# A linear attention kernel on one core: the first four pairs' output stored by eight software DMAs of 1 MB instead of four of 2 MB

## The chip, the core and the metric

The kernel runs on one core of a Trainium2 chip. The metric is the device time of one execution in microseconds (us), the median of three runs. Besides these there is one execution that was taken by the hardware profiler; everything that is said of single instructions and DMAs comes from that one.

## The reference, cut to what matters

Q, K and V are float32 arrays of 8 x 12 heads x 512 rows x 64 columns, 12.58 MB each; the output has the same shape. The computation is attention without a softmax:

```python
Q_feat = np.maximum(0, Q) + 1
K_feat = np.maximum(0, K) + 1
KV = np.einsum('bhkd,bhkv->bhdv', K_feat, V)
K_sum = np.sum(K_feat, axis=2)
numerator = np.einsum('bhqd,bhdv->bhqv', Q_feat, KV)
denominator = np.einsum('bhqd,bhd->bhq', Q_feat, K_sum)
return numerator / (denominator[:, :, :, None] + 1e-10)
```

Each head reads its K and V rows once, makes a small 64 x 64 matrix and a sum from them, and then multiplies its Q rows with that. Nearly every byte is read once and written once.

## The kernel before, in words

The 96 heads are worked on in six **pairs**, numbered 0 to 5, each of 16 heads: two blocks n = 0, 1 of eight heads each for K and V, and one block of 16 heads for Q and the output. For each pair the kernel loads K, V and Q, each 2 MB of float32 in DRAM, by software DMAs that POOL issues (`load`, line 142, and `load_q`, line 133); they become 1 MB of bf16 in SBUF. Only the very first block of K is loaded by SP (line 128). DVE makes the K features (line 159) and Q features (line 175); ACT and DVE copy V into a block form (line 171); PE accumulates K features times V (line 186), transposes Q (line 206) and makes the output sums and denominators (line 221); ACT moves results out of PSUM (lines 198 and 213); DVE takes the reciprocal of the denominators (line 234) and multiplies (line 235). This last step is `norms`; there are eight of them for a pair, parts 0 to 7, and each writes 256 KB of the float32 tile `o_sb`.

`o_sb` has four buffers (`OUT_BUFS`). The six pairs and the first K block, which borrows one, share them, so that the `norms` of pair 4 write the buffer from which pair 0 was stored, and those of pair 5 the buffer of pair 2. In the built program the first multiplication of pair 4 waits for pair 0's store, and that of pair 5 for pair 2's.

The order of the work is written out by hand: `ORDER` has a list of tasks for each engine. A task is a letter, the pair, and a part: `lv2` is the load of V of pair 2, `n37` the `norms` of pair 3, part 7, and `s40` the first store of pair 4. `trace_all` emits each engine's tasks in this order; `needs` only tells which other tasks must have been emitted before. `stores_of(s)` says into how many DMAs a pair's store is cut and which parts each takes; `store` (line 150) issues it. Pairs 0 to 3 are stored by one DMA of eight parts, pair 4 by two of four parts on POOL, and pair 5 by three on SP (four, two and two parts).

POOL's list ends with the loads of pair 5 and then the six stores of pairs 0 to 4, in the order of pairs 0, 2, 1, 3, 4, 4. No store is issued before the last load. POOL's DMAs all use one queue, q0, and eight completion semaphores in turn; the first K block and the stores of pair 5 use SP's queue, q1. The stores that POOL issues have the option `single_packet`. In DRAM a part has 2 KB runs, one for each of the 128 partitions.

Of the kernel before, what the change touches and what calls it, by code (L numbers as in the profile page):

```python
# [41 lines left out]
        v413 v411 e40 c41 c40 c43 c42 v500 c51 c50 e41 v511 v513 c52 e50 c53 e51  # L42
    """,
    POOL="""
        lv2 lk2 lq2 lv3 lq3 lk3 lq4 lv4 lk4 lv5 lq5 lk5 s00 s20 s10 s30 s40 s41
    """,
    SP="""
        s50 s51 s52
# [5 lines left out]
def kernel(  # L54
# [210 lines left out]
    last = NPAIR - 1  # L265
    done = set()

    def needs(engine, task):
# [34 lines left out]
        if x == "no":  # L303
            old = s - OUT_BUFS
            return [("om", s, at[0])] + [("st", old, j) for j in range(len(stores_of(old)))]
        if x == "st":
            return [("no", s, p) for p in stores_of(s)[at[0]]]

    def stores_of(s):

        if s < 0:
            return ()
        if s < last - 1:
            return (range(8),)
        return (range(4), range(4, 8)) if s < last else (range(4), range(4, 6), range(6, 8))

    def trace(engine, task):
        x, s, *at = task
        if x == "load":
            load(at[0], s)  # L320
        elif x == "kf":
            k_features(s, at[0])
        elif x == "vb":
            copy = nc.vector.tensor_copy if engine == "DVE" else nc.scalar.copy
            v_block(s, at[0], at[1], copy)
        elif x == "qf":
            q_features(s)
        elif x == "kv":
            keys_values(s, *at)
        elif x == "ev":  # L330
            weights(s, at[0])
        elif x == "tr":
            transposes(s, at[0])
        elif x == "tc":
            transposed(s, at[0], nc.vector.tensor_copy if engine == "DVE" else nc.scalar.copy)
        elif x == "om":
            out_matmuls(s, at[0])
        elif x == "no":
            norms(s, at[0])
        elif x == "st":  # L340
            store(s, stores_of(s)[at[0]], nc.sync if s == last else nc.gpsimd)
# [69 lines left out]
```

## Time and profile before

| | |
|---|---|
| median of 3 runs | 125.55 us (125.53 to 125.63) |
| the profiled execution's own time | 125.6 us |
| span of its instructions | 123.8 us |
| busy: DVE, ACT, PE, POOL | 72%, 72%, 67%, 15% of the span |
| DMA, mean rate over the span | 259 GB/s counted as written |
| HBM read and written | 37.75 MB and 12.58 MB |

The span goes from the first instruction to the last; the 1.8 us between it and the profiled execution's time lie outside the instructions. The page cuts the span into 40 slices of 3.1 us each and gives for each slice the busy share of every engine in tenths, the mean busy share of the 16 DMA engines and the rate. A loaded byte is counted as it is written, as bf16, so that a load stretch at 212 GB/s reads about 424 GB/s of float32. A DMA's time "to landing" goes from its issue to its last completion, and so holds all that it waited for behind other DMAs.

### The profile page before, as it was taken

What the parts mean: (1) busy time and instruction counts of PE and PEld (TensorE: products, weight loads), DVE (VectorE), ACT (ScalarE), POOL (GpSimd) and SP (SyncE); (2) the same over time, 40 slices, a digit from 0 to 9 for tenths busy, and PEclk for the clock granted to TensorE, in tenths of its full rate; (3) what the DMA queues carried; (4) which work ended last, traced back from release to release, by engine and by line L of the source; (5) the groups of instructions that cost most, each with busy time, mean ns of one, the idle gap of its engine ahead of it and who ended that gap; (6) DMA issues with size and microseconds to landing.
All of it is one profiled execution on the core that took longest, in us unless ns stands there. A gap on an engine that the chain in (4) does not pass through costs nothing.

```text
span 123.8 us, 2306 instructions
## 1 busy us (share of the span) xinstructions
PE 83.0 (67%) x960; PEld 62.7 (51%) x960; DVE 89.7 (72%) x167; ACT 89.3 (72%) x99; POOL 18.6 (15%) x32
## 2 busy tenths in 40 slices
PE   0000396881998957999919998399984999976000
PEld 0000275851676835688716776277853677654000
DVE  4795429609699599969569992999959789789200
ACT  7959914939969999399999559999992996540000
POOL 6900000600003200140000090050000200220000
PEclk9999999999599997699995999999999599997555
DMA  3999999999999999999999999999999999999992
GB/s 85 339 212 212 217 214 217 213 232 220 192 212 217 229 209 209 214 220 210 220 226 198 213 217 216 213 226 202 214 327 417 419 413 418 417 413 417 409 407 100
DMA packets 7897, 32.11 MB, mean 259 GB/s; under 512 B 464, under 2 KB 464, under 8 KB 6992
## 3 DMA queue, kind: packets, MB, share of 16 engines
q0 software_dynamic: 6672, 28.84, 93.6%
q1 hardware_dynamic: 1216, 3.15, 6.8%
q8 instruction: 7, 0.11, 0.3%
q14 instruction: 2, 0.02, 0.0%
HBM read 37.75 MB, written 12.58 MB: 406 GB/s over the span
## 4 chain that ended last, share of the span: by engine, by line
DMA 44%; DVE 14%; PE 14%; ACT 13%; issue 4%; POOL 3%; POOLq 0%
DMA k_raw<-in_K_dram 32%; DMA q_raw<-in_Q_dram 12%; PE kva_ps L186 10%; DVE o_sb L235 7%; ACT v_all L171 6%; ACT qt L213 5%; DVE kf L159 4%; PE o_ps L221 3%; ACT kva L198 2%; POOL v_raw L142 2%; DVE v_all L171 2%; DVE recip L234 1%; PE qt_ps L206 1%; DVE qf L175 1%; POOL q_raw L133 0%
## 5 line engine op out<-in xcount | busy, mean ns | idle before, releaser
L186 PE MATMUL kva_ps<-v_all,kf 128*128 128x260 bf16 x384 | 55.2, 297 | 20.7 <-DVE v_all L171 17.7
L186 PEld LDWEIGHTS <-kf 128*128 128x128 bf16 x384 | 37.7, 105 | 31.1 <-DVE v_all L171 16.3
L171 ACT COPY v_all<-v_raw 32x2048 bf16<-32x2048 bf16 x22 | 42.3, 1929 | 6.9 <-DMA v_raw<-in_V_dram 5.1
L235 DVE TENSOR_TENSOR o_sb<-o_ps,recip 128x512 f32<-128x512 f32 x48 | 33.2, 692 | 1.7
L213 ACT COPY qt<-qt_ps 128x1024 bf16<-128x1024 bf16 x24 | 23.5, 1014 | 10.9 <-PE qt_ps L206 8.3
L221 PE MATMUL o_ps<-kva,qt 128*64 128x130 bf16 x384 | 20.6, 238 | 9.6 <-DVE o_sb L235 9.0
L159 DVE TENSOR_SCALAR kf<-k_raw,shift,least 128x2048 bf16<-128x2048 bf16 x22 | 16.9, 810 | 8.0 <-DMA k_raw<-in_K_dram 8.0
L221 PEld LDWEIGHTS <-qt 128*64 128x64 bf16 x384 | 13.3, 116 | 18.0 <-DVE o_sb L235 11.9
L171 DVE COPY v_all<-v_raw 32x2048 bf16<-32x2048 bf16 x26 | 18.0, 692 | 5.9 <-DMA v_raw<-in_V_dram 5.3
L198 ACT CAST kva<-kva_ps 64x260 bf16<-64x260 f32 x48 | 17.9, 374 | 3.7 <-PE kva_ps L186 2.9
L206 PE MATMUL qt_ps<-identity,qf 128*128 128x128 bf16 x192 | 14.0, 220 | 1.1 <-ACT qt L213 0.6
L206 PEld LDWEIGHTS <-qf 128*128 128x128 bf16 x192 | 12.0, 99 | 2.5 <-issue 0.8
L142 POOL DMA_DIRECT2D v_raw<-in_V_dram x7 | 4.9, 701 | 49.1 <-ACT qt L213 18.1
L234 DVE RECIPROCAL recip<-o_ps 128x8 f32<-128x8 f32 x48 | 9.6, 201 | 3.2 <-PE o_ps L221 3.0
L175 DVE TENSOR_SCALAR qf<-q_raw 128x4096 bf16<-128x4096 bf16 x6 | 7.3, 1223 | 4.7 <-DMA q_raw<-in_Q_dram 4.6
L150 POOL DMA_DIRECT2D out_dram<-o_sb x6 | 5.1, 853 | 30.9 <-DVE o_sb L235 23.6
L258 DVE MEMSET v_all<- 128x2600 f32 x2 | 4.5, 2225 | 1.1 <-issue 1.1
L133 POOL DMA_DIRECT2D q_raw<-in_Q_dram x6 | 3.5, 580 | 10.5 <-DVE recip L234 10.5
L142 POOL DMA_DIRECT2D k_raw<-in_K_dram x6 | 4.5, 746 | 0.0
L259 ACT COPY v_all<-zero 128x1560 f32<-128x1560 f32 x2 | 3.0, 1488 | 0.0
L159 DVE TENSOR_SCALAR kf<-o_sb,shift,least 128x2048 bf16<-128x2048 f32 x2 | 2.6, 1358 | 0.0
L374 ACT COPY kva<-zero 128x1040 f32<-128x1040 f32 x2 | 2.0, 1052 | 0.0
(17 smaller groups left out, 4.6 us busy)
## 6 DMA issues: line engine op xcount, KB each, us to landing
out_dram<-o_sb POOLq DMA_DIRECT2D x4, 2048.0 KB, 22.8
q_raw<-in_Q_dram POOLq DMA_DIRECT2D x6, 1024.0 KB, 17.4
k_raw<-in_K_dram POOLq DMA_DIRECT2D x5, 1024.0 KB, 19.9
v_raw<-in_V_dram POOLq DMA_DIRECT2D x5, 1024.0 KB, 15.7
out_dram<-o_sb POOLq DMA_DIRECT2D x2, 1024.0 KB, 10.0
o_sb<-in_K_dram SPq DMA_DIRECT2D x1, 1024.0 KB, 4.8
v_raw<-in_V_dram POOLq DMA_DIRECT2D x2, 512.0 KB, 8.5
out_dram<-o_sb SPq DMA_DIRECT2D x1, 1024.0 KB, 8.3
```

What stands on the lines that cost most here:

```text
L142: nc.gpsimd.dma_start(out=t[:, ns[0] : ns[-1] + 1], in_=drams[x][:, 2 * s + ns[0] : 2 * s + ns[-1] + 1])
L150: engine.dma_start(out=o_dram[:, 8 * s + lo : 8 * s + hi], in_=outs[s][:, lo:hi], single_packet=engine is nc.gpsimd,)
L159: nc.vector.tensor_scalar(out=kf[:, :, a], in0=raw["k", s, n], scalar1=shift[:, a : a + 1], scalar2=least[:, a : a + 1], op0=ALU.add, op1= ...
L171: copy(out=v_alls[n][ps, :, b * D1 : b * D1 + D], in_=raw["v", s, n][ps])
L175: nc.vector.tensor_scalar(out=qf.rearrange("p r c d -> p (r c) d"), in0=raw["q", s], scalar1=1.0, scalar2=1.0, op0=ALU.add, op1=ALU.max,)
L186: nc.tensor.matmul(kva_pss[s, n], lhsT=kfs[s, n][:, c].rearrange("p a d -> p (a d)"), rhs=v_alls[n][:, c], start=(c == 0), stop=(c == ROWS ...
L198: nc.scalar.copy(out=kvas[s % 2][64 * x : 64 * x + 64, 8 * n + a : 8 * n + 8 : 2, x], in_=kva_ps[64 * a : 64 * a + 64].rearrange("p (b d) ...
L206: nc.tensor.transpose(qt_ps[:, r], qfs[s][:, r, 2 * i : 2 * i + 2].rearrange("p x d -> p (x d)"), identity)
L213: copy(out=qts[s][:, i], in_=qt_pss.pop((s, i)).rearrange("p r q -> p q r"))
L221: nc.tensor.matmul(o_ps[64 * t : 64 * t + 64, c // 2, (c % 2) * W : (c % 2) * W + W], lhsT=qts[s][:, c, 8 * h : 8 * h + 8], rhs=kvas[s % 2 ...
L234: nc.vector.reciprocal(out=recip, in_=cells[:, :, :, D:D1])
L235: nc.vector.tensor_tensor(out=outs[s][:, part].rearrange("p (b r) d -> p b r d", b=2), in0=cells[:, :, :, 0:D], in1=recip.to_broadcast([P, ...
```

## The change

Two places are changed. In POOL's list every one of the four stores of pairs 0 to 3 becomes two tasks that follow each other, and `stores_of` no longer gives those pairs one range of eight parts, so that they get the two ranges of four parts that pair 4 had already.

```diff
     POOL="""
-        lv2 lk2 lq2 lv3 lq3 lk3 lq4 lv4 lk4 lv5 lq5 lk5 s00 s20 s10 s30 s40 s41
+        lv2 lk2 lq2 lv3 lq3 lk3 lq4 lv4 lk4 lv5 lq5 lk5 s00 s01 s20 s21 s10 s11 s30 s31 s40 s41
     """,
...
     def stores_of(s):
 
         if s < 0:
             return ()
-        if s < last - 1:
-            return (range(8),)
         return (range(4), range(4, 8)) if s < last else (range(4), range(4, 6), range(6, 8))
```

The lists of the other engines, the bytes and their places in DRAM stay as they are. Lines behind `stores_of` have numbers that are smaller by two in the kernel after.

## The prediction

> **What bounds the kernel now.** I read the page's slices first, then its queues. No compute engine is over 72% busy, but the DMA row is at 9 (90% or more) in 38 of 40 slices:
>
> ```profile
> DMA  3999999999999999999999999999999999999992
> GB/s 85 339 212 212 217 214 217 213 232 220 192 212 217 229 209 209 214 220 210 220 226 198 213 217 216 213 226 202 214 327 417 419 413 418 417 413 417 409 407 100
> ...
> q0 software_dynamic: 6672, 28.84, 93.6%
> q1 hardware_dynamic: 1216, 3.15, 6.8%
> q8 instruction: 7, 0.11, 0.3%
> ...
> HBM read 37.75 MB, written 12.58 MB: 406 GB/s over the span
> ```
>
> Two stretches are to be seen: loads at about 212 GB/s (424 GB/s on the float32 side), and from slice 29 on, at 92 us, nothing but stores at 407 to 419 GB/s. At 417 GB/s the 50.3 MB alone take 120.7 us of the 123.8 us span. So I ask next when each store was issued and when it landed. This is POOL's timeline; its columns are start, duration, engine, line, operation, and in brackets the idle time before it and what ended that:
>
> ```profile
> 72.45 1.02 POOL L142 DMA_DIRECT2D k_raw<-in_K_dram  x1
> 73.47 0.92 POOL L150 DMA_DIRECT2D out_dram<-o_sb  x1
> 81.74 1.77 POOL L150 DMA_DIRECT2D out_dram<-o_sb  x2 [7.34 <-DVE recip L234]
> 97.44 0.90 POOL L150 DMA_DIRECT2D out_dram<-o_sb  x1 [13.94 <-DVE o_sb L235]
> 105.44 0.76 POOL L150 DMA_DIRECT2D out_dram<-o_sb  x1 [7.10 <-DVE o_sb L235]
> 108.73 0.75 POOL L150 DMA_DIRECT2D out_dram<-o_sb  x1 [2.52 <-DVE o_sb L235]
> ```
>
> The view of DMA issues, asked for a window round each single issue, gives its own time to landing: 24.4, 21.2, 25.3 (the longest that the tile's view has), 15.5, 10.0 and 10.0 us. Issue plus landing puts the last completions of the six at 97.9, 102.9, 107.9, 112.9, 115.4 and 118.7 us; the last load, K of pair 5, landed at 92.2 (72.45 + 19.8). **The stores therefore run one behind the other, 5.0 us for 2 MB**, and each was issued 5 to 23 us before the queue came to it. Pair 5's stores on SP follow: issued at 112.1 to 115.5 us, the last one landed 7.5 us later at 123.0. DVE's last multiplication ended at 115.4, so 7.6 us of pure DMA backlog end the program.
>
> The windows of 5 us through the stores say the same; the number before the last is the DMA share, the last is GB/s:
>
> ```profile
> 92.00:97.00 5.00, 2.60 (x27) 1.91 (x25) 4.60 (x9) 2.59 (x4) 0.00 (x0) 0.90 1.03 418
> 97.00:102.00 5.00, 5.00 (x61) 3.40 (x60) 4.00 (x9) 4.92 (x7) 0.90 (x1) 0.76 1.02 417
> 102.00:107.00 5.00, 4.88 (x64) 3.72 (x64) 4.19 (x11) 3.90 (x7) 0.76 (x1) 1.00 1.03 418
> 107.00:112.00 5.00, 4.22 (x64) 2.83 (x60) 4.64 (x12) 1.49 (x4) 0.75 (x1) 1.00 1.02 414
> ```
>
> There is no hole that a change of issue could fill. The end is set by the bytes in the queue and by what is lost at the borders between DMAs.
>
> **The change part by part.** Everything up to 73.47 us stays: POOL's list is the same up to the last load. Four stores of 2 MB become eight of 1 MB, in the same order of pairs and with the same bytes.
>
> *Borders in the queue.* Four more borders stand on the path that sets the end. The nearest row is pair 4, which is stored in two halves already: pair 3's 2 MB landed 5.0 us after the store before it, and pair 4's first 1 MB 2.53 us after that, by the last of the 16 engines (2.49 by the first). Half of a 2 MB step is 2.48 to 2.53 us (steps of 4.95, 5.06 and 5.02). A border then costs between 2.49 - 2.53 = -0.04 and 2.53 - 2.48 = +0.05 us. Loads say the same: the three half loads at the start (512 KB each in SBUF) landed at 8.1, 10.5 and 13.0 us, 2.46 apart, the full ones 4.87 to 4.90 apart, so +0.02 a border. The trace's packet records add one completion record of 9 ns for each engine and store. I take 0.02, as the loads had nothing else beside them: 4 x 0.02 = **+0.08 us**, bounds 4 x -0.04 = -0.16 and 4 x 0.05 = +0.20.
>
> The Trainium skill ("DMA: Bandwidth & Descriptors", the anatomy of one software DMA) speaks against the change here: about 2.0 us fixed for each DMA, plus its bytes at 436 GB/s. By that rule, added up, four more DMAs would cost 8 us; the page also says that most of it is the wait for the write's receipt, and the row above, 2.5 us for 1 MB and 5.0 for 2 MB, shows that next to none of it is paid between DMAs that are queued behind each other.
>
> *POOL's issues.* A 2 MB store holds POOL for 0.89 to 0.92 us, a 1 MB one for 0.75 and 0.76: 8 x 0.76 - 4 x 0.90 = +2.5 us of POOL, spread from 73 to 98 us. Behind them in POOL's list stand only pair 4's stores. The issue of pair 3's second half stays at about 97.4 us (its parts are finished no earlier), when the queue still has pair 1 to do until 107.9; pair 4's halves wait for DVE at 105.4 and 108.7 as before and are needed at 112.9 and 115.4. The cover is 10, 7 and 6 us, so the issues cost 0.
>
> *Waits.* Eight semaphores are used in turn, so four more DMAs shift which earlier DMA each store must have seen landed. The built program has pair 1's second half wait for the load of V, pair 3's halves for Q and K of pair 5, and pair 4's for pair 0's halves. These landed, or will, at 82.4, 87.3, 92.2, 95.4 and 97.9 us; the queue needs these stores 105 us or later. What is queued behind such a wait on POOL is only the following stores, with the covers above: 0. On DVE the first multiplication of pair 4 waits for both of pair 0's halves instead of its one store. It started at 98.64 us, while pair 0 landed at 97.9:
>
> ```profile
> 98.40 0.21 DVE L234 RECIPROCAL recip<-o_ps 128x8 f32<-128x8 f32 x1 [0.54 <-PE o_ps L221]
> 98.64 0.69 DVE L235 TENSOR_TENSOR o_sb<-o_ps,recip 128x512 f32<-128x512 f32 x1
> ```
>
> That is 0.7 us of slack against a shift of 0.02. If it were gone, pair 4's and 5's `norms` would move with it, and the first to be missed is pair 5's first store: issued at 112.1, its turn in the queue comes with the end of pair 4 on the earliest engine at 116.1. About 2 us of it are free even if a DMA from SP takes 2 us to get going (the lone K load at the start landed 4.8 us after its issue, 2.5 us of which are 1 MB at the stores' rate). So this costs 0 up to a slip of 0.7 + 2 us. Pair 5's first multiplication waits for pair 2's halves, landed at 102.9, and started at 108.86.
>
> *DVE beside POOL's issues.* One copy on DVE took 0.86 us where two issues ran at 81.7 to 83.5 us, against 0.69 else. Four more issues might cost DVE 4 x 0.17 = 0.7 us, off the path by the same 2 us: 0.
>
> **Sum.** 123.83 + 0.08 = 123.9 us span; 125.60 + 0.08 = 125.68 on the profiled execution's scale. The median of the runs is 0.05 below it, so I say **125.65 us**, no change that could be told: a measurement of this kernel tells about 0.2% (0.25 us) from nothing. Bounds of the border alone: 125.4 to 125.85.
>
> **The rivals.**
>
> *Slower: an instruction block on the last engine.* The landing events show that the 16 DMA engines do not end together: for the last store the first ended at 121.15, the next to last at 122.48, the last at 122.96. In the packet records PE's seven instruction blocks of 16 KB (q8 above) take 0.94 to 0.98 us each, and where one ran, at 27.7 and at 94.8 us, the last engine fell back by about 0.8 us (a step of 5.74 instead of 4.9, and of 5.66 instead of 5.0). The change adds instructions on POOL and waits on DVE. If one more block is fetched over the engine that ends last, the end is +0.8 us: 126.4. It decides if POOL's or DVE's program crosses into another block; for it speaks that the end hangs on one engine, against it that POOL had no later block with some 60 instructions and PE's stream is unchanged. 0.12.
>
> *Faster: the same, the other way.* If a block moves off that engine, the next to last decides: 122.96 - 122.48 = 0.5 us less, 125.1. I see no reason for a move but cannot see how engines are chosen: 0.06.
>
> *Slower: the borders drain.* If the queue went on only after a store's completion, each border would cost what the lone load had on top of its bytes, 4.8 - 2.5 = 2.3 us, and four 9.2 us: 134.8. Pair 3 to pair 4 speaks against it: 0.03.
>
> *Slower: the late halves.* DVE's wait slips past 2.7 us, each further us is paid: about 126.5. 0.03.
>
> *Faster: buffers come free sooner.* The halves land 2.5 us earlier for their first parts, but the wait is for both, and DVE ended 7.6 us before the end: nothing to win; 0.02 for 125.2.
>
> *The change does not do what it says.* Stores merged or cut otherwise: the built program has ten stores of four parts on POOL, so 0.02, and 125.55.
>
> **How the numbers follow.** The forecast has 0.72. With the last rival, within 0.2% has 0.74; faster by more 0.06 + 0.02 = 0.08; slower by more 0.12 + 0.03 + 0.03 = 0.18. The range must leave out no more than 0.2, so it takes the forecast's bounds and reaches up to the instruction block: 125.35 to 126.4.
>
> **What would show it.** Right: eight store issues of 1024 KB before 98 us, landings 2.5 us apart from 92.2 us on, GB/s at 410 to 420 up to slice 37, DVE's multiplication of pair 4 not released by a DMA. Wrong: store steps of 2.6 us or more, a hole in the DMA row behind 92 us, q8 or q14 with more packets, or the same steps with one engine that ends 0.8 us later.

## The result and the profile after

| | before | after |
|---|---|---|
| median of 17 runs each | 125.5 us | 125.72 us |
| ratio after to before | | 1.0024, 95% interval 1.0015 to 1.0033 |
| span of the profiled execution | 123.83 us | 123.76 us |
| its own time | 125.6 us | 125.73 us |

The change is slower: by 0.22 us between the medians and by 0.24% (0.30 us) in the ratio. That lies about at the 0.2% which the prediction took as the bound of "no change"; the interval of 0.15 to 0.33% leaves out zero. The median is 0.07 us above the 125.65 foretold and inside the range. But the span did not grow: it was 123.68 us on average in the 17 runs after, while the kernel before averaged 123.65 to 123.79 us on the three chips of the experiments below. What grew is the part of the time that lies outside the span.

The page after has the same picture in the stores' stretch as the page before, slices of 3.1 us, and then the queues and the issues:

```profile
DMA  3999999999999999999999999999999999999992
GB/s 106 328 211 221 220 200 216 212 230 214 203 213 216 221 214 209 225 217 203 224 222 200 213 217 212 214 222 207 216 322 420 410 421 418 409 414 420 408 407 103
...
q0 software_dynamic: 6736, 28.84, 93.7%
...
q14 instruction: 2, 0.02, 0.0%
...
out_dram<-o_sb POOLq DMA_DIRECT2D x10, 1024.0 KB, 21.2
```

There is no hole in the DMA row, and the rate through the stores (407 to 421 GB/s) is that of before. q0 has 64 packets more: four DMAs times 16 engines, the completion records. POOL's timeline after (start, duration, engine, line, operation, idle before):

```profile
73.20 2.33 POOL L150 DMA_DIRECT2D out_dram<-o_sb  x3
81.78 2.24 POOL L150 DMA_DIRECT2D out_dram<-o_sb  x3 [6.25 <-DVE recip L234]
92.56 0.79 POOL L150 DMA_DIRECT2D out_dram<-o_sb  x1 [8.54 <-DVE o_sb L235]
97.50 0.75 POOL L150 DMA_DIRECT2D out_dram<-o_sb  x1 [4.15 <-DVE o_sb L235]
104.57 0.75 POOL L150 DMA_DIRECT2D out_dram<-o_sb  x1 [6.32 <-DVE o_sb L235]
107.86 0.75 POOL L150 DMA_DIRECT2D out_dram<-o_sb  x1 [2.53 <-DVE o_sb L235]
```

With the landing of each issue the first half of pair 0 landed at 94.7 us (73.20 + 21.5), 2.5 after the last load; pair 3's halves at 110.4 (92.56 + 17.8) and 112.8 (97.50 + 15.3), and pair 4's first at 115.3 (104.57 + 10.7). Most 1 MB steps take 2.5 us, half of a 2 MB step; two of the eight, beside blocks of PE's program, take 2.9 and 2.7 us by the last of the 16 engines. The last store landed at 122.9 us, before at 123.0. DVE's multiplication for pair 4 was released by no DMA, as forecast:

```profile
97.95 0.21 DVE L234 RECIPROCAL recip<-o_ps 128x8 f32<-128x8 f32 x1
98.19 0.69 DVE L235 TENSOR_TENSOR o_sb<-o_ps,recip 128x512 f32<-128x512 f32 x1
```

Queues 8 and 14 carry the engines' programs, in blocks: q8 has PE's in packets of 16 KB, q14 those of other engines in packets of 8 KB. Inside the span q14 has the same line before the change:

```profile
q14 instruction: 2, 0.02, 0.0%
```

What is new lies behind the last instruction at 123.76 us. The view of the DMA queues, asked for the window 123.5 to 128 us, has for the kernel before

```profile
DMA packets 0, 0.00 MB, mean 0 GB/s; under 512 B 0, under 2 KB 0, under 8 KB 0
```

and for the kernel after one packet of instructions (8 KB; it started at 125.64 us and took 0.34):

```profile
DMA packets 1, 0.01 MB, mean 2 GB/s; under 512 B 0, under 2 KB 0, under 8 KB 0
## 3 DMA queue, kind: packets, MB, share of 16 engines
q14 instruction: 1, 0.01, 0.5%
```

The page does not show it, since it ends with the span. Each run gives its time and its span (this one to 0.1 us). Time minus span is 2.08 us on average in the 17 runs after, 1.92 at the least; in the profiled execution before it is 1.77.

The lengths of the built programs fit this. An instruction takes 64 bytes there, and POOL's program grew from 61 of them (3904 bytes) to 67 (4288 bytes), by four DMAs and two waits on semaphores. Those of the other engines kept their length (DVE 185, ACT 121).

### The profile page after: what moved, and what is told of

Same layout as the page of the kernel before. It is cut to its first block, busy times and chain, and to the rows that moved or that the text cites. A ratio compares the mean times of both kernels' runs of the same rounds, so it can differ in the third digit from the quotient of the medians.

```text
span 123.8 us, 2312 instructions
## 1 busy us (share of the span) xinstructions
PE 84.1 (68%) x960; PEld 63.2 (51%) x960; DVE 89.5 (72%) x167; ACT 89.2 (72%) x99; POOL 20.8 (17%) x36
## 4 chain that ended last, share of the span: by engine, by line
DMA 48%; DVE 25%; issue 9%; PE 7%; POOL 3%; POOLq 0%; DVEq 0%
DMA k_raw<-in_K_dram 30%; DMA v_raw<-in_V_dram 18%; DVE o_sb L235 11%; DVE v_all L171 6%; PE kva_ps L186 6%; DVE kf L159 5%; DVE recip L234 2%; PE o_ps L221 2%; POOL v_raw L142 1%; POOL k_raw L142 1%; DVE qf L175 1%; POOL q_raw L133 1%; POOL identity masks.py:199 0%; POOL identity masks.py:197 0%; POOL lane L361 0%
## 5 line engine op out<-in xcount | busy, mean ns | idle before, releaser
L186 PE MATMUL kva_ps<-v_all,kf 128*128 128x260 bf16 x384 | 56.5, 302 | 20.5 <-DVE v_all L171 17.8
L186 PEld LDWEIGHTS <-kf 128*128 128x128 bf16 x384 | 38.3, 106 | 31.2 <-DVE v_all L171 16.3
L221 PE MATMUL o_ps<-kva,qt 128*64 128x130 bf16 x384 | 20.1, 233 | 8.1 <-DVE o_sb L235 7.4
L150 POOL DMA_DIRECT2D out_dram<-o_sb x10 | 7.6, 766 | 27.8 <-DVE o_sb L235 21.5
```

The lines of the kernel that those rows point to most:

```text
L150: engine.dma_start(out=o_dram[:, 8 * s + lo : 8 * s + hi], in_=outs[s][:, lo:hi], single_packet=engine is nc.gpsimd,)
L186: nc.tensor.matmul(kva_pss[s, n], lhsT=kfs[s, n][:, c].rearrange("p a d -> p (a d)"), rhs=v_alls[n][:, c], start=(c == 0), stop=(c == ROWS ...
L221: nc.tensor.matmul(o_ps[64 * t : 64 * t + 64, c // 2, (c % 2) * W : (c % 2) * W + W], lhsT=qts[s][:, c, 8 * h : 8 * h + 8], rhs=kvas[s % 2 ...
```

## The experiments

**Theory A**: the added time is a matter of the length of POOL's program: it ends near the place where one more block of instructions is asked for, and that is paid behind the last instruction, whatever the stores do. **Theory B**: the borders between the added DMAs cost it. All runs were timed against the kernel before on the same chip, in three groups of four. On these chips the kernel before had time minus span between 1.73 and 1.85 us in all of 90 runs (means of 1.78, 1.79 and 1.79), so that a step of 0.2 to 0.4 us stands out in a single run. In the table a **pad** is a number of idle instructions added to the kernel before; "after" stands for the kernel after.

| run | POOL instructions | ratio to before | 95% interval | mean time minus span | runs above 1.9 |
|---|---|---|---|---|---|
| pad, 6 memsets | 67 | 1.0015 | 1.0004 to 1.0026 | 2.02 | 8 of 11 |
| 512 KB stores | 78 | 1.0032 | 1.0020 to 1.0043 | 2.12 | 6 of 6 |
| one pair split | 63 | 1.0031 | 1.0019 to 1.0042 | 2.18 | 6 of 6 |
| after, again | 67 | 1.0017 | 1.0004 to 1.0030 | 2.04 | 9 of 11 |
| after, cut back | 61 | 1.0005 | 0.9992 to 1.0017 | 1.80 | 0 of 12 |
| pad, 2 memsets | 63 | 1.0040 | 1.0023 to 1.0056 | 2.19 | 9 of 9 |
| pad, 40 memsets | 101 | 1.0012 | 1.0001 to 1.0024 | 1.77 | 0 of 11 |
| pad on DVE and ACT | 61 | 1.0013 | 0.9999 to 1.0027 | 1.97 | 10 of 12 |
| after, 34 memsets | 101 | 0.9997 | 0.9983 to 1.0011 | 1.78 | 0 of 12 |
| pad, 17 memsets | 78 | 1.0004 | 0.9988 to 1.0020 | 1.79 | 0 of 12 |
| pad, 1 memset | 62 | 1.0025 | 1.0008 to 1.0042 | 2.00 | 12 of 12 |
| pad on ACT | 61 | 1.0013 | 1.0000 to 1.0026 | 1.78 | 0 of 12 |

The last two columns carry the verdicts. The ratios also hold the span, which scatters by some tenths of a us from run to run.

### First group: length or borders

*Six memsets on POOL, stores as before.* The memsets write columns of a tile that nobody reads; POOL is idle there.

```diff
+    pad = const.tile([P, 8], FP32, name="pad")
...
         for x in "kvq":
             load(x, 1)
+        for i in range(6):
+            nc.gpsimd.memset(pad[:, i : i + 1], 0.0)
         clear(1)
```

> The kernel before, with six one-column memsets added to POOL's list ahead of its first waiting load, so that POOL's program is as long as in the kernel after (67 instructions instead of 61) while the stores stay at 2 MB. Theory A (the added time is one more 8 KB instruction block, fetched once POOL's program is long enough, behind the last instruction): +0.2 to +0.3 us against the kernel before, all of it outside the span, and one instruction packet behind 124 us. Theory B (the borders between the added store DMAs cost it): within 0.1 us of the kernel before, no such packet.

Eight of the 11 runs had 2.06 to 2.15 us outside the span, three 1.74 to 1.83. The profiled execution was one of the three, and its trace has no packet behind the end. So the same step comes without any change to the stores, but not in every run.

*Stores of 512 KB.* `stores_of` gives pairs 0 to 3 four ranges of two parts, and POOL's list has four tasks for each.

```diff
+        if s < last - 1:
+            return tuple(range(i, i + 2) for i in (0, 2, 4, 6))
...
-        ... s00 s01 s20 s21 s10 s11 s30 s31 s40 s41
+        ... s00 s01 s02 s03 s20 s21 s22 s23 s10 s11 s12 s13 s30 s31 s32 s33
+        s40 s41
```

> Pairs 0 to 3 are stored by sixteen DMAs of 512 KB: twelve borders more than before instead of four. Theory A: the span grows by 12 x 0.01 to 0.02 = 0.1 to 0.25 us, and outside the span the same +0.2 to +0.3 us as in the kernel after. Theory B: three times what the kernel after lost, +0.6 to +0.9 us, in the span, with steps of 1.30 us or more between the landings of neighbouring stores instead of 1.25.

With three times as many added borders, the span averaged 123.72 us, against 123.68 for the kernel before on that chip: a difference of 0.04 us for twelve borders, which the scatter of the spans hides (standard error 0.035). In the trace the 512 KB stores landed 1.25 to 1.27 us apart on average of the engines, a quarter of 5.0, save for two steps of 1.36 beside blocks of PE's program. The landings give a sharper figure: from the last load to the last store of pairs 0 to 3 they took, on average of the 16 engines, 20.30 to 20.34 us in the eight traces with 2 MB stores, 20.33 and 20.34 in the three with 1 MB stores and the same stores of pair 4, and 20.38 here. Four borders cost at most 0.04 us by that, and twelve 0.04 to 0.08, less than the 0.1 to 0.25 that the expectation allowed even under theory A. Theory B falls. The loss was about the same as with four borders, and outside the span. One thing did not fit theory A: POOL's extra block was fetched at 121.7 us, ahead of the end, and the time was lost all the same. The third group comes back to this.

*Only pair 0 in two halves.*

```diff
-        if s < last - 1:
+        if 0 < s < last - 1:
             return (range(8),)
```

> Only pair 0 is stored by two DMAs of 1 MB (POOL's program has 63 instructions, between 61 before and 67 after). Theory A: either nothing or the whole +0.2 to +0.3 us, depending on where the threshold lies, and the instruction packet behind 124 us goes with it. Theory B: a quarter of what the kernel after lost, +0.06 us, no packet.

With one added border as much was lost as with four or twelve: 2.16 to 2.20 us lay outside the span in all six runs, and the span was 123.63 us. But no instruction packet is recorded behind the end, so that part of the expectation missed.

*The kernel after again.*

> The kernel after itself, on the same chip as the other three. Both theories: +0.2 to +0.3 us against the kernel before; theory A: with the span equal within 0.1 us, and the instruction packet behind 124 us; theory B: with a longer span.

The span was 123.61 us against 123.68. Time minus span was 2.03 to 2.15 us in nine runs of 11 and 1.81 and 1.82 in two, and the packet was there again, at 125.27 us in an execution whose span ended at 123.40.

### Second group: shorter, longer, and other engines

*The kernel after with POOL's program cut back to 61.* The mask of partitions that POOL's iota gave is summed by DVE from the identity, DVE clears the identity, and SP issues pair 4's stores.

```diff
-        nc.gpsimd.iota(lane, pattern=[[0, 1]], base=0, channel_multiplier=1)
...
-            store(s, stores_of(s)[at[0]], nc.sync if s == last else nc.gpsimd)
+            store(s, stores_of(s)[at[0]], nc.sync if s >= last - 1 else nc.gpsimd)
```

> The eight 1 MB stores of the kernel after, with POOL's program cut back to the 61 instructions of the kernel before: the partition mask is summed by DVE from the identity instead of POOL's iota, DVE clears the identity, and pair 4's two stores are issued by SP. Theory A (the added time hangs on the length of POOL's program, outside the span): the difference between time and span is 1.78 us as before, not 2.1, and the time is that of the kernel before to 0.1 us unless pair 4's other queue moves the span, which the span shows. Theory B (it hangs on the number of store DMAs): the difference stays at 2.1 us.

All 12 runs lay between 1.77 and 1.82 us outside the span: with the eight 1 MB stores in place, the loss is gone. DVE keeps its 185 instructions in this kernel; SP's grow from 23 to 26, without a loss. The span was 123.75 against 123.65; since pair 4 takes another queue here, I do not read that difference.

*Two memsets on POOL* (the pad with `range(2)`).

> The kernel before with two memsets added on POOL (63 instructions, as many as with one pair split). Theory A: time minus span 2.1 to 2.2 us in most executions, as with one pair split; the span unchanged. Theory B: 1.78 us in all.

Time minus span was 2.13 to 2.25 us in all nine runs, the same as with one pair split, which has the same number of instructions. Here too no packet is recorded behind the end.

*Forty memsets on POOL.*

> The kernel before with forty memsets added on POOL (101 instructions). Theory A in the form that a second block of POOL's program has to be there at all: time minus span 2.1 us. Theory A in the form that this block comes too late: it is fetched far earlier, and the difference falls back to 1.78 us. Theory B: 1.78 us.

Time minus span was 1.73 to 1.83 us in all 11 runs. In the trace an 8 KB block is fetched at 43.03 us that the kernel before does not fetch there. So a further block does not cost by being there; what theory A has left is that it is asked for at the very end. The ratio of 1.0012 is in the span (123.79 against 123.65); I have no cause for it.

*Six instructions more on DVE and six on ACT, POOL at 61.*

> The kernel before with six instructions added on DVE and six on ACT, and POOL's 61 as they were. Theory A: nothing (1.78 us outside the span). A wider theory, that any engine's longer program costs it: 2.1 us. Theory B: nothing.

Time minus span was 1.97 us on average, and an 8 KB block was fetched at 125.51 us, behind the end. So theory A was too narrow: it need not be POOL. The trace points to DVE: a block on q14 that comes at 39.3 to 39.7 us in the other 13 traces, that with ACT alone padded among them, came at 36.8 us here.

### Third group: the kernel after with the block in the middle

*The kernel after with 34 memsets.*

> The kernel after with thirty-four memsets more on POOL (101 instructions), so that the next block of POOL's program is fetched in the midst of the kernel, as it was near 43 us with forty memsets on the kernel before. Theory A (the block is asked for near the program's end and waited for there): although POOL does more, time minus span falls from 2.1 to 1.78 us and the time to that of the kernel before within 0.1 us. Theory B (the number of store DMAs costs it): 2.1 us, +0.25 us against before.

This is the run that decides between the two theories. Its eight stores are those of the kernel after, its POOL program is longer still by 34 instructions, and it is as fast as the kernel before: 0.9997 (0.9983 to 1.0011), time minus span 1.72 to 1.82 in all 12 runs. The view of the DMA queues in the window 30 to 122.9 us has one instruction packet on q14 more than the kernel after has there (2):

```profile
q14 instruction: 3, 0.02, 0.1%
```

and behind the end, 123.5 to 128 us, it has none:

```profile
DMA packets 0, 0.00 MB, mean 0 GB/s; under 512 B 0, under 2 KB 0, under 8 KB 0
```

The block came at 55.36 us instead, beside the loads, and nothing of it is left outside the span.

*Seventeen memsets: 78 instructions, stores of 2 MB.*

> The kernel before with seventeen memsets on POOL: 78 instructions, as many as with the stores of 512 KB, which lay at 2.1 us outside the span although their block was fetched at 121.7 us, ahead of the end. If the length of POOL's program sets it alone: 2.1 us here too, and a block fetched late in the span. If the finer stores had a cost of their own: 1.78 us here.

Time minus span was 1.73 to 1.85 us in all 12 runs, with the block at 121.75 us. So 78 instructions on POOL cost nothing, and the loss with 512 KB stores has another source. By the expectation that is a cost of the finer stores themselves, and no run rules it out for sixteen of them. But in that kernel DVE's program is longer too: 187 instead of 185, since the first multiplications of pairs 4 and 5 wait for four stores each. By the pad on DVE and ACT a longer DVE program can cost it as well. That this is the source is argued from the two, not shown by a run with DVE alone two instructions longer.

*One memset: 62 instructions.*

> The kernel before with one memset on POOL (62 instructions), between 61, with 1.78 us outside the span in all executions, and 63, with 2.19 in all. Theory A with a sharp threshold: either 1.78 or 2.1 to 2.2 us in nearly all executions, not something between for all. Theory B: 1.78 us.

Time minus span was 1.96 to 2.04 us in all 12 runs: one instruction is enough. It is between the two values that a sharp threshold would have given. The kernel before stood at the last free length ahead of this stretch. No packet behind the end is recorded here either.

*Six instructions more on ACT alone.*

> The kernel before with six instructions more on ACT only (127), POOL and DVE as before. With six on DVE and six on ACT, time minus span was 1.97 us on average and a block was fetched behind the end. If it is ACT's program, which comes close to 128 instructions: 1.9 to 2.1 us again and an instruction packet behind 124 us. If it was DVE's: 1.78 us and no packet.

Time minus span was 1.74 to 1.82 us in all 12 runs, and there is no packet: ACT alone is not it, which leaves DVE for the run with both. The ratio of 1.0013 is in the span again (123.96 against 123.79), without a cause that I know.

Taken together, with DVE at 185 instructions, time minus span by the length of POOL's program is 1.78 to 1.80 us at 61, 2.00 at 62, 2.18 and 2.19 at 63, 2.02 to 2.08 at 67, and 1.77 to 1.79 again at 78 (stores of 2 MB) and 101. The traces have POOL's further block the later the shorter the program is: at 43 and 55 us with 101 instructions, at 121.7 with 78, at 125.27 and 125.64 in two of the three with 67, and not at all with 61 to 63.

## Why the prediction came out as it did

*What bounds the kernel, and the borders.* This part was right in kind: the stores ran one behind the other as before, and the span did not grow beyond its scatter of some tenths of a us (123.9 foretold, 123.76 measured). The term of +0.08 us, 0.02 for each border, was at least twice too high: by the landings four borders made at most 0.04 us. One reading was loose: the landings that the prediction gives have each store issued 7 to 20 us ahead of its turn, not 5 to 23, and nothing hangs on it. Of the 2.0 us fixed for each DMA (the Trainium skill, "DMA: Bandwidth & Descriptors", the anatomy of one software DMA) next to nothing was paid between DMAs that stand in a queue. No run here shows what is paid at its end.

*POOL's issues, the waits, DVE.* They stood at nothing in the sum, and so it was: pair 4's issues came at 104.57 and 107.86, no multiplication waited for a store, and DVE ended 0.9 us earlier than before without any gain, for the last landing stayed at 122.9.

*The step that was wrong* is in the sum: "123.83 + 0.08 = 123.9 us span; 125.60 + 0.08 = 125.68". It carried the 1.8 us between span and time over unchanged, as if nothing that a change does could reach it. It measured 2.08 on average in the runs after, against 1.78 before, and these 0.3 us are the whole loss. That 125.65 came so near to 125.72 all the same is in part luck: the sum began at 125.55, 0.05 above the later median of 17 runs, and added a border cost that was hardly there. Neither has to do with what made the kernel slower.

*The rival with the instruction block* had the cause half right. It named more instructions and one more block, but looked for the price on the DMA engine that ends last (0.8 us inside the span), and it argued against itself that "POOL had no later block with some 60 instructions". Some 60 was just the wrong length: 61 is free, 62 is not. One of the signs of being wrong that the prediction named, "q8 or q14 with more packets", did come, but behind the span. The other rivals (draining borders, late halves, sooner buffers) did not happen.

The Trainium skill ("Runtime: NRT & Kernel Launch", on the mechanics of instruction fetch) has instructions refilled in blocks of 16 KiB while the engine runs, with crossing a block mostly hidden. PE's seven blocks of 16 KB agree with the size, and the block in the middle of the run with 34 memsets with the crossing being hidden. The blocks on q14 here are of 8 KB, and the three executions that recorded one behind the end had 0.2 to 0.4 us more outside the span than the kernel before.

*What stays open.* Shown is that the loss comes and goes with the length of POOL's program, whatever the stores do. That it is the wait for a block of instructions is argued: which instruction waits behind the span is not in the trace. With 62 and 63 instructions the time is lost and no packet is recorded; whether it comes after the record's end I cannot tell, nor why with 61 nothing is lost. Nor do I know why two of 11 repeats of the kernel after, and three of 11 with six memsets, escaped.

## What to carry to other kernels

Where the time of two kernels differs by a few tenths of a us, compare time minus span before looking for a cause inside: if the span is equal, the loss lies outside it. A change that only adds a few instructions to an engine can cost that much by where its program then ends. Adding some idle instructions shows it, and here it also takes the loss away. Cutting a queued store into halves or quarters costs next to nothing as long as the queue never runs empty.

## What the runs showed that I had not expected

More work can be faster: the kernel after with 34 useless memsets has 1.78 us outside the span, without them 2.04 to 2.08.

POOL's eight completion semaphores, used in turn, hold it back once the DMAs are small. With 512 KB stores POOL waited for earlier DMAs to land, which it did neither in the kernel before nor in the kernel after:

```profile
82.57 0.73 POOL L151 DMA_DIRECT2D out_dram<-o_sb  x1 [4.17 <-DMA v_raw<-in_V_dram]
87.72 1.02 POOL L151 DMA_DIRECT2D out_dram<-o_sb  x1 [4.42 <-DMA q_raw<-in_Q_dram]
92.62 0.73 POOL L151 DMA_DIRECT2D out_dram<-o_sb  x1 [3.89 <-DMA k_raw<-in_K_dram]
```

The name in brackets is the DMA whose landing let POOL go on: that of V, Q and K of pair 5, eight DMAs earlier. Eight stores of 512 KB are some 10 us of the queue (8 x 1.25), so the queue did not run empty.
